# Where the second unit's key products and the inverses' steps are called in a hybrid decoder kernel

## The chip, the cores and the metric

The kernel runs on one core of a Trainium2 chip. The metric is the device time of one execution in microseconds (us). The core has five engines with a queue of instructions each: TensorE (PE in the profile, its weight loads PEld), VectorE (DVE), ScalarE (ACT), GpSimd (POOL) and SyncE (SP), whose queue issues the DMAs. Each queue is worked off in order; semaphores let one engine wait for another or for a DMA. Results of TensorE land in PSUM banks, everything else lies in SBUF.

## What is computed

Two layers, each with three branches over the same normalised input: a state space mixer (SSD), latent attention (MLA) and a gated delta net (GDN). Each branch is projected, gated and summed; then come an output projection and a feed-forward part. The change concerns the delta net's preparation, which runs beside the state space branch's projection:

```python
def gated_delta_chunked(q, k, v, g, beta):
    ...
    decay = jnp.exp(jnp.where(incl, g[..., :, None] - g[..., None, :], -jnp.inf))
    kb = k * beta[..., None]
    a_mat = jnp.where(strict, jnp.einsum('bhcld,bhcmd->bhclm', kb, k) * decay, 0.0)
    rhs = jnp.concatenate([v * beta[..., None], kb * jnp.exp(g)[..., None]], axis=-1)
    sol = lax.linalg.triangular_solve(a_mat + jnp.eye(L, dtype=jnp.float32), rhs,
                                      left_side=True, lower=True)
...
def hybrid_layer(...):
    ...
    mixed = g_ssd * (y_ssd @ w_ssd_out) + g_mla * (y_mla @ w_mla_out) + g_gdn * (y_gdn @ w_gdn_out)
    h = x + mixed @ w_out
```

The sequence has 512 tokens and the model 1024 channels. The delta net has 8 value heads on 4 key heads; its products of keys with keys (`a_mat`) have to be inverted before the scan over the sequence can start.

## The kernel before

Every large product is done three times with operands split into a high and a low part (`mm3`, lines L182 to L184), so that the sum of three fast matmuls has nearly full precision. The split of weights is a cast on ScalarE (`whi`, L154) and a subtraction on VectorE (`wlo`, L155), both ranked as urgent. Weights come by DMA into `wraw` (two buffers, L161); `whi` and `wlo` have four buffers each.

`dense_F` walks the weights of one product in pieces of two blocks of 128 input channels. For two column tiles of 128 it then issues 2 x 2 x 3 = 12 matmuls of 128x128 by 128x512. One such piece is called a row here. After each row `dense_F` calls the function given as `after`. `out_proj` runs, for each of four pieces `dp` of 256 channels, the gate's product (four rows, operand `xh`/`xl`) and the branch's projection (four rows, operand `yh`/`yl`), 32 rows in all. For the state space projection `after` is `between`, which counts the rows from 0. The delta net's query product of unit 0 (`key_tiles(2 * u, between)` in `gdn_unit`) has four more rows, 32 to 35, that call it too.

The delta net's eight heads are done in two units of four. `gdn_matrix(u)` consists of

- `key_tiles`: the product for two key tiles, then convolution and SiLU (ScalarE and VectorE) into `ft`;
- the products of keys with keys (L834, 128x128), evacuated into `wk0` to `wk3` (L838, L839);
- their norms: a power on POOL (L843) and a few short operations on VectorE;
- 16 products with the decays, which are loaded into `eE` (L854), into `nt` (tag `tok`, L857), and four stores of its diagonal blocks to `d_n` (L861).

`gdn_blocks` loads the blocks of both units (L873) and inverts them by 31 steps of two operations each on VectorE (L879, L880). It stores the result and its transpose to `d_x` and `d_y` (L885) and loads them back in another order into `wk` (L888). `gdn_inverse` returns nine closures, the steps: `first` for each unit (64 small matmuls at L913, from `wk`), `second` for each unit (L929, L930) and five of `last_doubling` (L949, L951). `between` calls one of them behind each row from a given one on.

No engine's order is written out by hand. The program is traced as it is written, and a scheduler then orders each engine's instructions ahead of time: an instruction's rank is its place in the program (raised for code in `tc.high_priority()`), and the scheduler takes, engine by engine, the instruction of best rank among those whose inputs and buffers it expects to be ready by its own estimate of durations. The order is fixed from then on; on the chip an engine whose next instruction has no data yet waits.

Of the kernel before, what the change touches and what calls it, by code (L numbers as in the profile page):

```python
# [55 lines left out]
def hybrid_kernel(ctx, tc, a, out, depth=2, taps=None):  # L56
# [4 lines left out]
    def mk(pl, shape, dt, tag, bufs=None):  # L61
        return pl.tile(shape, dt, tag=tag, name=f"{tag}_{next(uid)}", bufs=bufs)
# [8 lines left out]
    def bc_mid(ap, n):  # L71
        sh = list(ap.shape)
        return ap.unsqueeze(1).to_broadcast([sh[0], n] + sh[1:])

    def bc_last(ap, n):
        sh = list(ap.shape)
        return ap.unsqueeze(len(sh)).to_broadcast(sh + [n])
# [15 lines left out]
    def sm_bank():  # L93
        return mk(ps_sm, [P, 512], F32, "sm")
# [70 lines left out]
    def weights(w2d, c0, n, K, hold=None, raw0=None):  # L165

        kt = min(1024 // n, K // P)  # L170
        step = 512 // n
        for k0 in range(0, K // P, kt):
            given = raw0 is not None and k0 == 0
            raw = raw0 if given else weights_raw(w2d, c0, n, k0, kt)
            for q in range(0, kt, step):
                hi, lo = split_half(raw[:, q * n : (q + step) * n], hold and hold[k0 + q], not given)
                v = lambda x: x.rearrange("p (k n) -> p k n", n=n)
                yield k0 + q, v(hi), v(lo)
# [7 lines left out]
    def dense_F(gen, cols, K, xh, xl, mid=None, banks=None, after=None):  # L186

        pss = banks or [acc_bank() for _ in cols]
        last = K // P - 1
        if mid:
            gen = list(gen)
            for i, hf in enumerate(HALVES):
                for ps, c in zip(pss, cols):
                    for k0, wh, wl in gen:
                        for k in range(wh.shape[1]):  # L200
                            kk = k0 + k
                            mm3(ps[:, hf], wh[:, k, c], wl[:, k, c], xh[kk][:, hf], xl[kk][:, hf], kk == 0, kk == last)
                if i == 0:
                    mid()
            return pss
        for k0, wh, wl in gen:
            for ps, c in zip(pss, cols):
                for k in range(wh.shape[1]):
                    a_, b_ = wh[:, k, c], wl[:, k, c]
                    mm3(ps[: a_.shape[1], :], a_, b_, xh[k0 + k], xl[k0 + k], k0 + k == 0, k0 + k == last)  # L210
            if after:
                after()
        return pss

    def tiles(n):
        return [slice(i, i + P) for i in range(0, n, P)]
# [134 lines left out]
    for ly in range(depth):  # L351
# [198 lines left out]
        for hp in range(4):  # L550
# [67 lines left out]
            for j in range(2):  # L618
# [3 lines left out]
                for t in range(T):  # L622
                    n = max(256, (t + 1) * P)
# [9 lines left out]
                    n = (t + 1) * P  # L633
# [11 lines left out]
                for kbs in ((0,), (1,), (3, 2)):  # L645
                    ps = sm_bank()
                    n = 0
# [158 lines left out]
        def gconv_silu(ps, c, o):  # L806
            conv_silu(ps, [gconv(j, c) for j in range(4)], None, o)

        def key_tiles(c0, after=None):

            res = [mk(br, [P, S], F32, "ft", 6) for _ in range(2)]
            for i, ps in enumerate(dense_F(weights(w_in, O_GQ + c0 * P, 256, D), tiles(256), D, xh, xl, after=after)):
                gconv_silu(ps, c0 + i, res[i])
            return res
# [6 lines left out]
                    seg_exp(e, t, 16 + 4 * u)  # L821
                    sync.dma_start(d_e[u, t], e)

        def gdn_matrix(u):

            hd0 = 16 + 4 * u
            kT = key_tiles(4 + 2 * u)
            ssq = mk(sp, [P, 2, T], F32, "gss", 2)
            gks = []
            for t in range(T):  # L830
                tok = slice(t * P, (t + 1) * P)
                pg = sm_bank()
                for i in range(2):
                    pe.matmul(pg[:, i * P : (i + 1) * P], kT[i][:, tok], kT[i][:, tok], start=True, stop=True)  # L834
                gk = mk(br, [P, 2, P], F32, f"wk{t}")
                for i in range(2):

                    dve.scalar_tensor_tensor(gk[:, i], hv(pg)[:, i], 1.0, ident, ALU.mult, ALU.mult, accum_out=ssq[:, i, t : t + 1])  # L838
                dve.tensor_tensor(gk, hv(pg)[:, 0:2], bc_mid(nstrict, 2), ALU.mult)  # L839
                gks.append(gk)  # L840
            dve.tensor_scalar(ssq, ssq, 4.0 * EPS, None, ALU.add)
            ork = mk(sp, [P, 2, T], F32, "gork", 2)
            pool.tensor_tensor(ork.rearrange("p i t -> p (i t)"), ssq.rearrange("p i t -> p (i t)"), phalf[:, :8], ALU.pow)  # L843
            dve.tensor_scalar(ork, ork, 0.5, None, ALU.mult)
            rk2 = mk(sp, [P, 2, T], F32, "grk", 2)
            dve.reciprocal(rk2, ssq)
            cc = mk(sp, [P, T, 4], F32, "gcc", 2)
            for i in range(2):
                dve.tensor_tensor(cc[:, :, 2 * i : 2 * i + 2], beta[:, :, 4 * u + 2 * i : 4 * u + 2 * i + 2],
                                  bc_last(rk2[:, i, :], 2), ALU.mult)  # L850
            nt = mk(br, [P, T, 4, P], F32, "tok", 5)
            for t in range(T):
                e = mk(br, [P, 4, P], F32, "eE", 4)
                sync.dma_start(e, d_e[u, t])  # L854
                gk = gks[t]
                for h in range(4):
                    dve.scalar_tensor_tensor(nt[:, t, h], e[:, h], cc[:, t, h : h + 1], gk[:, h // 2], ALU.mult, ALU.mult)  # L857
            ntf = nt.rearrange("p t h n -> p (t h) n")
            for b in range(4):
                sl = slice(32 * b, 32 * b + 32)  # L860
                sync.dma_start(d_n[u][:, b].rearrange("h i j -> i h j"), ntf[sl, :, sl])  # L861
            cd = mk(sp, [P, T, 4], F32, "gcd", 2)
            dve.tensor_tensor(cd, cc, dec[:, 1, :, hd0 : hd0 + 4], ALU.mult)
            return kT, ork, cc, cd, nt

        def gdn_blocks():

            wk = mk(br, [P, 2, 32, 32], F32, "tok", 5)
            nb, xb = wk[:, 0], wk[:, 1]
            sync.dma_start(nb, d_n.rearrange("u h b i j -> (u h b) i j"))  # L873
            xf = xb.rearrange("p i j -> p (i j)")
            pool.memset(xf, 0.0)
            pool.memset(xf[:, ::33], 1.0)
            for m in range(31):
                pd = mk(br, [P, 31 - m, m + 1], F32, "gQ", 2)
                dve.tensor_tensor(pd, bc_last(nb[:, m, m + 1 :], m + 1), bc_mid(xb[:, m, : m + 1], 31 - m), ALU.mult)  # L879
                dve.tensor_tensor(xb[:, m + 1 :, : m + 1], xb[:, m + 1 :, : m + 1], pd, ALU.add)  # L880
            xbt = nb
            dve.tensor_copy(xbt, xb.rearrange("p i j -> p j i"))
            res = [[], []]
            for i, (src, d_) in enumerate(((xb, d_x), (xbt, d_y))):
                sync.dma_start(d_.rearrange("u h b i j -> (u h b) i j"), src)  # L885
                for u in range(2):
                    c = mk(br, [P, 16, 32], F32, f"wk{2 * i + u}")
                    sync.dma_start(c, d_[u].rearrange("h b i j -> (b i) h j"))  # L888
                    res[u].append(c)
            return res  # L890
# [70 lines left out]
        def gdn_unit(u, kT, ork, cc, cd, Yt, yh, yl):  # L961
            hd0 = 16 + 4 * u
            qT = key_tiles(2 * u, between)
            pss = sm_bank()
            for i in range(2):
# [111 lines left out]
        ssd_group(1, *ys)  # L1077
        out_proj(a["w_mla_out"][ly], 1, *y_mla, br, (2, 3))
        d_n, d_x, d_y = (mk(dr, [2, 16, 4, 32, 32], F32, n, 2) for n in ("d_n", "d_x", "d_y"))
        mats = [gdn_matrix(u) for u in range(2)]  # L1080
        blocks = gdn_blocks()
        steps = gdn_inverse([m[4] for m in mats], blocks)

        rows = itertools.count()

        def between():
            if next(rows) >= 24 and steps:
                steps.pop(0)()

        out_proj(a["w_ssd_out"][ly], 0, *ys, br, after=between)  # L1090
        yg = hilo_tags(lp, "y")
        for u in range(2):
# [312 lines left out]
```

## Time and profile before

| | us |
|---|---|
| median of three timed executions | 2307.58 |
| their range | 2307.19 to 2308.72 |
| the profiled execution's own time | 2309.95 |
| its span, first to last instruction | 2308.2 |
| mean granted TensorE clock in it | 0.996 |

In the views of the trace a line of the timeline gives the start and the duration in us, the engine, the line of the program, the operation, output<-input and a count. In square brackets stand the idle time of the engine ahead of it and what ended that time. A line of the waits gives who waited for whom, then the total in us, the number of times and the longest. The granted clock is a share of full speed.

### The profile page before, as it was taken

Reading aid. Unit: us, or ns where it says so; the run is one execution under the profiler, and the core shown is the slowest. Engines: PE = TensorE matmul, PEld = TensorE weight load, DVE = VectorE, ACT = ScalarE, POOL = GpSimd, SP = SyncE. Lnnn points to the kernel's source line nnn. Section 1 sums busy time; section 2 is a strip of 40 time slices with the busy share of each in tenths; the row PEclk is TensorE's granted clock in tenths of the full one; section 3 lists DMA queues with packets and bytes.
Section 4 is the critical chain, followed back from the end, with each engine's and each line's share of the span. In section 5 each row is a group of like instructions: output and inputs, shape, how many; then the busy total and the mean of one; then the engine's idle time right before and its main releaser. Section 6 shows DMA issues by size and latency. Waiting matters only on the chain.

```text
span 2308.2 us, 32276 instructions
## 1 busy us (share of the span) xinstructions
PE 2272.9 (98%) x11810; PEld 1867.7 (81%) x11810; DVE 1645.9 (71%) x3256; ACT 1202.0 (52%) x2509; POOL 59.4 (3%) x74
## 2 busy tenths in 40 slices
PE   9999999999999999999999999999999999999998
PEld 8888787878887888888888887878788877888886
DVE  7777566875666778767867765668657667778668
ACT  6766644333443455554657666443334435645545
POOL 0000000000000000000000000000000000000000
PEclk9999999999999999999999999999999999999999
DMA  4223633442223233233132236334422241432231
GB/s 142 80 74 101 192 101 119 131 126 83 78 78 134 95 137 110 75 117 119 47 103 79 71 110 192 101 110 146 120 82 83 65 164 55 152 113 101 92 110 46
DMA packets 220032, 244.16 MB, mean 106 GB/s; under 512 B 34256, under 2 KB 172384, under 8 KB 219872
## 3 DMA queue, kind: packets, MB, share of 16 engines
q1 hardware_dynamic: 219872, 242.09, 33.3%
q8 instruction: 93, 1.52, 0.3%
q14 instruction: 67, 0.55, 0.1%
HBM read 225.60 MB, written 11.74 MB: 103 GB/s over the span
## 4 chain that ended last, share of the span: by engine, by line
PE 88%; DVE 6%; ACT 1%; DMA 1%; POOL 1%; issue 1%; SPq 0%; DVEq 0%; POOLq 0%; ACTq 0%
PE acc L182 22%; PE acc L183 22%; PE acc L184 22%; PE sm L182 3%; PE sm L184 3%; PE sm L183 3%; DVE wlo L155 2%; PE sm L752 1%; DVE tok L880 1%; PE sm L650 1%; DVE gQ L879 1%; PE sm L761 1%; PE sm L1037 1%; POOL gms L259 1%; ACT whi L154 1%
## 5 line engine op out<-in xcount | busy, mean ns | idle before, releaser
L154 ACT CAST whi<-wraw 128x512 fp32r<-128x512 f32 (+1 forms) x536 | 329.9, 618 | 546.1 <-PE acc L183 382.7
L155 DVE TENSOR_TENSOR wlo<-wraw,whi 128x512 fp32r<-128x512 f32 (+1 forms) x536 | 365.2, 686 | 347.9 <-ACT whi L154 341.4
L184 PE MATMUL acc<-xh,wlo 128*128 128x512 f32 (+1 forms) x1344 | 523.9, 390 | 0.0
L182 PE MATMUL acc<-xh,whi 128*128 128x512 f32 (+1 forms) x1344 | 523.4, 390 | 0.0
L183 PE MATMUL acc<-xl,whi 128*128 128x512 f32 (+1 forms) x1344 | 523.0, 389 | 0.0
L183 PEld LDWEIGHTS acc<-xl,whi 128*128 128x128 f32 x1344 | 253.7, 189 | 48.3 <-DVE xl L255 0.7
L184 PEld LDWEIGHTS acc<-xh,wlo 128*128 128x128 f32 x1344 | 253.6, 189 | 47.9
L182 PEld LDWEIGHTS acc<-xh,whi 128*128 128x128 f32 x1344 | 253.3, 189 | 48.1 <-ACT xh L254 0.4
L154 ACT CAST whi<-wr 128x512 fp32r<-128x512 f32 x168 | 104.3, 621 | 107.8 <-PE acc L183 47.7
L183 PE MATMUL acc<-yl,whi 128*128 128x512 f32 x384 | 151.4, 394 | 0.0
L182 PE MATMUL acc<-yh,whi 128*128 128x512 f32 x384 | 150.7, 396 | 0.0
L184 PE MATMUL acc<-yh,wlo 128*128 128x512 f32 x384 | 149.9, 390 | 0.0
L155 DVE TENSOR_TENSOR wlo<-wr,whi 128x512 fp32r<-128x512 f32 x168 | 113.2, 686 | 35.6 <-ACT whi L154 34.7
L691 DVE SCALAR_TENSOR_TENSOR ckl<-acc,pc,ckl 128x511 f32<-128x511 f32 (+2 forms) x168 | 120.3, 743 | 15.5 <-ACT ckl L687 8.2
L182 PEld LDWEIGHTS acc<-yh,whi 128*128 128x128 f32 x384 | 71.6, 188 | 16.1 <-ACT yh L254 1.7
L184 PEld LDWEIGHTS acc<-yh,wlo 128*128 128x128 f32 x384 | 72.2, 188 | 14.5
L183 PEld LDWEIGHTS acc<-yl,whi 128*128 128x128 f32 x384 | 72.2, 188 | 13.8
L183 PE MATMUL acc<-wlo,xh 128*128 128x512 f32 (+1 forms) x208 | 79.9, 384 | 0.0
L184 PE MATMUL acc<-whi,xl 128*128 128x512 f32 (+1 forms) x208 | 79.5, 384 | 0.0
L182 PE MATMUL acc<-whi,xh 128*128 128x512 f32 (+1 forms) x208 | 79.5, 384 | 0.0
L1145 DVE TENSOR_TENSOR h<-h,acc 128x512 f32<-128x512 f32 x120 | 76.9, 679 | 0.1
L454 ACT ACTIVATE eE<-eE,cum 128x128 f32<-128x128 f32 x192 | 63.1, 390 | 22.7 <-DMA eE<-d_c 19.7
(453 smaller groups left out, 4552.2 us busy)
## 6 DMA issues: line engine op xcount, KB each, us to landing
wraw<-in_w_in_dram SPq DMA_DIRECT2D x144, 512.0 KB, 3.4
wraw<-in_w_up_dram SPq DMA_DIRECT2D x64, 512.0 KB, 3.6
wr<-in_w_down_dram SPq DMA_DIRECT2D x32, 1024.0 KB, 5.0
eE<-d_c SPq DMA_DIRECT2D x48, 256.0 KB, 4.0
wraw<-in_w_mla_out_dram SPq DMA_DIRECT2D x16, 512.0 KB, 3.3
eE<-d_e SPq DMA_DIRECT2D x32, 256.0 KB, 2.8
wraw<-in_w_ssd_out_dram SPq DMA_DIRECT2D x16, 512.0 KB, 3.3
wraw<-in_w_gdn_out_dram SPq DMA_DIRECT2D x16, 512.0 KB, 3.3
```

The lines of the kernel that those rows point to most:

```text
L154: act.copy(hi, raw)
L155: dve.tensor_tensor(lo, raw, f32(hi), ALU.subtract)
L182: pe.matmul(o, ah, bh, start=start, stop=False, skip_group_check=more)
L183: pe.matmul(o, ah, bl, start=False, stop=False, skip_group_check=more)
L184: pe.matmul(o, al, bh, start=False, stop=stop, skip_group_check=more)
L259: pool.tensor_tensor(o, o, (exp if exp is not None else nhalf)[:, : o.shape[1]], ALU.pow)
L454: act.activation(o[:, i], o[:, i], AF.Relu, scale=-1.0, bias=cum[:, t, h0 + i : h0 + i + 1])
L650: pe.transpose(ps[:, n : n + P], pn[t][:, kb * P : (kb + 1) * P], ident)
L691: dve.scalar_tensor_tensor(acc[:, d:], ps[:, : S - d], taps_[3 - d], acc[:, d:], ALU.mult, ALU.add)
L752: pe.matmul(py[64 * i : 64 * i + 64, c * P : (c + 1) * P], xd[:, t, h * 64 : (h + 1) * 64], e2[h // 4][:, h % 4, :], start=True, stop=True)
L761: pe.matmul(po[:, c * P : (c + 1) * P], st[:, c * P : (c + 1) * P], ctl[:, tok], start=True, stop=True)
L1145: dve.tensor_tensor(hs_, hs_, ps[t], op)
```

## The change

The second unit's key tiles are still computed ahead of the projection, right behind the first unit's matrix. The rest of the second unit's matrix, the inversion of the blocks and the making of the steps are called from `between` behind row 1, that is, from within the projection. The steps are called from row 26 on instead of row 24, so that the nine lie behind rows 26 to 34 instead of 24 to 32. What is computed stays the same.

```diff
-        def gdn_matrix(u):
+        def gdn_matrix(u, kT):
 
             hd0 = 16 + 4 * u
-            kT = key_tiles(4 + 2 * u)
             ssq = mk(sp, [P, 2, T], F32, "gss", 2)
...
-        mats = [gdn_matrix(u) for u in range(2)]
-        blocks = gdn_blocks()
-        steps = gdn_inverse([m[4] for m in mats], blocks)
+        mats = [gdn_matrix(0, key_tiles(4))]
+        k1 = key_tiles(6)
+        steps = []
 
         rows = itertools.count()
 
         def between():
-            if next(rows) >= 24 and steps:
+            n = next(rows)
+            if n == 1:
+                mats.append(gdn_matrix(1, k1))
+                steps.extend(gdn_inverse([m[4] for m in mats], gdn_blocks()))
+            if n >= 26 and steps:
                 steps.pop(0)()
```

## The prediction

> **What bounds the kernel now.** I read the page first, then the waits of TensorE, then the order of its instructions around the change in both layers, then the granted clock in short stretches.
>
> ```profile
> span 2308.2 us, 32276 instructions
> PE 2272.9 (98%) x11810; PEld 1867.7 (81%) x11810; DVE 1645.9 (71%) x3256; ACT 1202.0 (52%) x2509; POOL 59.4 (3%) x74
> ...
> PE 88%; DVE 6%; ACT 1%; DMA 1%; POOL 1%; issue 1%; SPq 0%; DVEq 0%; POOLq 0%; ACTq 0%
> ```
>
> TensorE is busy 2272.9 of 2308.2 us and has 88% of the chain that ended last. The change adds and removes no matmul, so it can win only what TensorE stands idle, or runs slow, near the moved code. Its waits there are two kinds:
>
> ```profile
> PE sm L913 <- DMA wk<-d_x: 2.7, 2, 1.8
> ...
> PE sm L834 <- DVE ft L263: 1.7, 2, 0.8
> ```
>
> L913 is the first step of the inverses (once in each layer it waits, 2.7 us in all); L834 is the second unit's key products (0.84 us in each layer). I number the projection's rows from 0, as the counter does. Layer 0 around the first step:
>
> ```profile
> 484.69 0.39 PE L182 MATMUL acc<-yh,whi 128*128 128x512 f32 x1
> ...
> 495.57 0.39 PE L182 MATMUL acc<-xh,whi 128*128 128x512 f32 x1
> ...
> 499.65 0.39 PE L182 MATMUL acc<-xh,whi 128*128 128x512 f32 x1
> 501.79 1.49 PE L913 MATMUL sm<-wk,tok 32*32 32x32 f32 x64 [1.76 <-DMA wk<-d_x]
> 503.21 0.80 PE L183 MATMUL acc<-xl,whi 128*128 128x512 f32 x1
> ...
> 505.64 1.92 PE L913 MATMUL sm<-wk,tok 32*32 32x32 f32 x64
> 507.49 0.80 PE L182 MATMUL acc<-xh,whi 128*128 128x512 f32 x1
> ...
> 512.84 0.22 PE L929 MATMUL sm<-wk,ft 32*32 32x32 f32 x2
> ```
>
> The operand changes from yh to xh where a gate product starts, every four rows. From 484.69 (row 20) to 495.57 (row 24) are 48 matmuls in 10.88 us: **0.2267 us a matmul, 2.72 us a row** of 12. So row 24 ends at 498.29, and the step, called behind row 24, stands 7 matmuls into row 25 ((499.65 - 498.29) / 0.2267 + 1). The second L913 stands 5 matmuls later, just behind row 25, and L929 12 later, behind row 26: these at their own calls. An instruction thus stands at its call, or later if its inputs were expected later. The same place in layer 1:
>
> ```profile
> 1646.61 0.39 PE L182 MATMUL acc<-xh,whi 128*128 128x512 f32 x1
> 1647.96 1.20 PE L913 MATMUL sm<-wk,tok 32*32 32x32 f32 x64 [0.96 <-DMA wk<-d_x]
> 1649.09 0.50 PE L183 MATMUL acc<-xl,whi 128*128 128x512 f32 x1
> ...
> 1654.52 0.22 PE L929 MATMUL sm<-wk,ft 32*32 32x32 f32 x2
> ```
>
> The same work, from the first L913 to the first L929, takes 512.84 - 501.79 = 11.05 us in layer 0 and 1654.52 - 1647.96 = 6.56 us in layer 1. Busy time in stretches (busy us and count of PE, PEld, DVE, ACT, POOL, then the granted clock) says why:
>
> ```profile
> 500.00:501.79 1.79, 0.03 (x1) 0.00 (x0) 0.00 (x0) 0.02 (x1) 0.00 (x0) 1.00 0.86 138
> 501.79:503.21 1.42, 1.42 (x64) 1.35 (x65) 0.00 (x0) 1.22 (x2) 0.00 (x0) 0.74 1.23 194
> 503.21:505.64 2.43, 2.43 (x9) 1.49 (x5) 0.70 (x1) 1.51 (x3) 0.00 (x0) 0.50 1.08 170
> ...
> 512.84:516.90 4.06, 4.06 (x110) 3.27 (x109) 1.37 (x2) 2.19 (x5) 0.00 (x0) 1.00 0.01 4
> ...
> 1648.00:1650.45 2.45, 2.45 (x70) 1.91 (x70) 0.64 (x1) 2.39 (x5) 0.00 (x0) 1.00 1.26 198
> ```
>
> Behind layer 0's idle time the clock falls to 0.50 until about 512.8; in layer 1 it stays at 1.00. The wait of 1.76 us therefore drags **11.05 - 6.56 = 4.49 us** behind it.
>
> What the step waits for, on VectorE and SyncE's queue:
>
> ```profile
> 455.07 0.33 SPq L873 DMA_DIRECT2D tok<-d_n  x1
> 461.44 0.18 DVE L879 TENSOR_TENSOR gQ<-tok 128x31 f32<-128x31 f32 x1
> ...
> 492.80 0.18 DVE L880 TENSOR_TENSOR tok<-tok,gQ 128x31 f32<-128x31 f32 x1
> 493.38 0.45 SPq L885 DMA_DIRECT2D d_x<-tok  x1
> 498.25 2.26 SPq L888 DMA_DIRECT2D wk<-d_x  x2
> 501.77 0.62 ACT L907 COPY tok<-wk 32x512 f32<-32x512 f32 x1 [2.89 <-DMA wk<-d_x]
> 505.32 0.62 ACT L154 CAST whi<-wraw 128x512 fp32r<-128x512 f32 x1 [0.78 <-PE acc L183]
> ```
>
> 31 steps on VectorE, a store at 493.38, the load issued at 498.25 and landed by 501.77: 8.4 us of round trip, and TensorE waits at its end.
>
> **The change part by part.** First, **the key products of unit 1** are called behind row 1 instead of ahead of row 0. Where they stand now:
>
> ```profile
> 433.11 0.39 PE L184 MATMUL acc<-xh,wlo 128*128 128x512 f32 x1
> 434.34 0.94 PE L834 MATMUL sm<-ft 128*128 128x128 f32 x6 [0.84 <-DVE ft L263]
> ...
> 440.71 0.39 PE L182 MATMUL acc<-yh,whi 128*128 128x512 f32 x1
> ```
>
> Row 4 starts at 440.71 (xh to yh); 21 of the 48 matmuls of rows 0 to 3 lie between L834 and that, so 27 lie ahead: the products already stand 3 matmuls behind the end of row 1. Their call moves past 24 matmuls that run ahead of them anyway, so I expect the same place and take 0. Bounds: the wait of 0.84 us vanishes in both layers (-1.68), or everything behind slips by two rows (the last rival). What else it issues, queue by queue:
>
> ```profile
> 399.61 17.01 SPq L161 DMA_DIRECT2D wraw<-in_w_in_dram  x4
> 421.53 9.32 SPq L161 DMA_DIRECT2D wraw<-in_w_ssd_out_dram  x2
> ...
> 436.05 2.42 SPq L854 DMA_DIRECT2D eE<-d_e  x3
> ...
> 446.59 0.99 POOL L906 MEMSET tok<- 32x512 f32 x2
> ```
>
> On SP it moves 4 loads of eE, 4 stores to d_n, and with the blocks the load of d_n, 2 stores and 4 loads of wk, all past one weight load, that of rows 0 and 1. The two loads at 421.53 and later are those of rows 4 to 7, so the last two of the four before them, issued by 416.6, are those of rows 0 to 3: nearly 20 us ahead of unit 1's first eE load at 436.05. This order stays as well: 0. POOL gets the power of L843 and the clearings; the L906 clearing belongs to the first step, called behind row 24, and yet ran at 446.59, 55 us ahead of the step. A call's place ranks work that is ready at the same time; it doesn't hold back work alone in its queue.
>
> Second, **the steps begin behind row 26.** The first L913 moves by the 5 matmuls left of row 25 and the 12 of row 26: 17 x 0.2267 = 3.85 us. Without waiting TensorE is free for it in layer 0 at 501.79 - 1.76 + 3.85 = 503.88 us, and the data, whose chain does not depend on TensorE's place, is there at 501.79: 2.1 us to spare. Layer 1: 1647.96 - 0.96 + 3.85 = 1650.85 against 1647.96, 2.9 to spare. So both waits go, and the slow stretch with them:
> 1.76 + 0.96 + 4.49 = **7.21 us**.
>
> On ScalarE the copies of L907 stay where they are ready, at 501.77, with the casts for coming rows queued behind. The cast at 505.32 is row 29's (whi has four buffers, so a cast follows the row four ahead of its own). It and VectorE's 0.69 us are over by some 507. With the change TensorE reaches row 29 at 503.88 + 1.13 + 2.72 + 1.13 + 2.72 + 1.1 = 512.7. Some 5 us of cover, so 0; were it gone, the excess would be a wait of TensorE.
>
> **The late end.** The nine steps now lie behind rows 26 to 34; three instead of one fall into unit 0's query product. Layer 1, where the last step now stands:
>
> ```profile
> 1678.78 1.14 PE L951 MATMUL sm<-tok,kt 64*64 64x64 f32 x16
> 1679.85 0.50 PE L182 MATMUL acc<-xh,whi 128*128 128x512 f32 x1
> ...
> 1695.18 0.95 PE L969 MATMUL sm<-ct,ft 128*128 128x1 f32 x8
> ```
>
> Two rows on, that step starts near 1679.85 + 5.44 = 1685.3, some 10 us ahead of L969, the first work of the unit after its query product, which waits for the query's convolution. The cost is 0 while the rows cover it; without them the last step and its copy, about 1.14 + 0.6 = 1.7 us a layer, would be in sight.
>
> The sum against the profiled execution's own time is 2309.95 - 7.21 = 2302.74 us (span 2300.97). That execution lies 2.37 us above the median 2307.58; on the median the forecast is **2300.4 us** (-0.31%).
>
> **The rivals.**
> (1) **Timed runs without the slow stretch.** The clock fell in one layer of two, so it may be a matter of chance. The three times, 2307.19 to 2308.72, lie closer than 4.49, so they all have it or all lack it. If they lack it, 1.76 + 0.96 = 2.72 is won: **2304.9**. For it: layer 1 at 1.00 after 0.96 us. Against it: the profiled execution without the stretch would be at 2305.46, 2.1 below the timed ones, which would make profiling a gain.
> The Trainium skill, "TensorE: Matmul & The Clock Gate", Part 1, states that the clock is cut after about 3.4 us without work, in a window that runs free of the kernel. By its length 1.76 us would not cut the clock and only 2.72 us could be won; the row with 0.50 disagrees, and the free window would leave each run to chance.
> (2) **Given back.** The wait goes, but one of the later steps, now among query rows, meets a wait that idles TensorE as long as this one: 1.76 + 4.49 return in one layer, 0.96 stays won: **2306.6**. For it: VectorE and ScalarE take their work in order. Against it: steps remain one row apart.
> (3) **The chain slips (slower).** If unit 1's products and all behind them do move by two rows, the data lands 5.44 us later, at 507.23 and 1653.40, against TensorE at 503.88 and 1650.85: waits of 3.35 and 2.55 us, each long enough for a slow stretch. 3.35 + 2.55 + 2 x 4.49 = 14.88 instead of 7.21: **2315.3**. It decides from a slip of 2.1 us on in layer 0. For it: the call is written behind row 1. Against it: the products already stand behind row 1.
>
> **How the numbers follow.** The forecast has 0.56, rival 1 0.24, rival 2 0.09, rival 3 0.11. The likeliest case alone runs from 2298.7 (the 1.68 of L834 won too) to 2301.9; the range goes on over rivals 1 and 2 to 2307.5 and leaves out rival 3 and some tails. About 0.2% (4.6 us) is what a measurement of this kernel tells from no change: the forecast lies beyond it, rivals 1 and 2 within, rival 3 beyond on the other side. With the tails: faster 0.55, same 0.35, slower 0.10.
>
> **What would show it.** Right: no wait of L913 for wk in either layer, the first L913 behind 12 more full matmuls of row 26, clock 1.00 throughout that stretch, L834 still 27 matmuls into the projection, a span near 2301. Wrong: a later start of the 31 steps relative to row 4, or a clock of 0.50 anywhere past the start, or a new wait of TensorE in the query rows.

## The result and the profile after

| | before | after |
|---|---|---|
| median of 20 timed runs, us | 2310.12 | 2305.23 |
| mean of them, us | 2310.25 | 2305.29 |
| lowest and highest, us | 2306.89, 2314.17 | 2303.88, 2307.16 |
| span of the profiled execution, us | 2308.2 | 2303.2 |

The ratio is 0.9978, with a 95% interval from 0.9972 to 0.9984: faster by 4.9 us. The three times known ahead (median 2307.58) lie in the lower part of the 20.

TensorE's waits after (who waited for whom, us in total, times, longest), where the loads of `wk` had 2.7 us:

```profile
PE sm L1017 <- DVE tok L1014: 3.5, 8, 0.5
...
PE sm L833 <- DVE ft L263: 1.7, 2, 0.8
```

No line of the list names `wk` any more; the wait of the key products is what it was (the changed kernel's lines from 833 on are numbered one lower). TensorE's timeline of the changed kernel, layer 0:

```profile
435.85 0.94 PE L833 MATMUL sm<-ft 128*128 128x128 f32 x6 [0.84 <-DVE ft L263]
...
505.31 1.20 PE L912 MATMUL sm<-wk,tok 32*32 32x32 f32 x64
506.44 0.50 PE L182 MATMUL acc<-xh,whi 128*128 128x512 f32 x1
...
509.39 1.20 PE L912 MATMUL sm<-wk,tok 32*32 32x32 f32 x64
510.52 0.50 PE L182 MATMUL acc<-yh,whi 128*128 128x512 f32 x1
```

There is no bracket at L912: the step no longer waits. The second one is followed by yh, that is, it stands at the end of row 27. ScalarE's timeline there:

```profile
503.17 0.62 ACT L906 COPY tok<-wk 32x512 f32<-32x512 f32 x1 [2.79 <-DMA wk<-d_x]
503.80 0.62 ACT L907 COPY tok<-wk 32x512 f32<-32x512 f32 x1
504.45 0.62 ACT L154 CAST whi<-wraw 128x512 fp32r<-128x512 f32 x1
```

The data is there at 503.17, TensorE comes at 505.31: 2.14 us to spare, where 2.1 were worked out. The cast that is queued behind the copies runs at 504.45. Busy times and granted clock of the same place (the columns as in the prediction):

```profile
500.00:505.31 5.31, 5.31 (x24) 4.13 (x22) 0.90 (x2) 2.48 (x5) 0.00 (x0) 1.00 0.92 155
505.31:510.52 5.21, 5.21 (x142) 4.36 (x141) 2.86 (x6) 4.54 (x8) 0.00 (x0) 1.00 1.03 250
510.52:525.00 14.48, 14.48 (x259) 11.65 (x255) 6.74 (x10) 6.38 (x11) 0.00 (x0) 1.00 0.28 81
```

TensorE is busy throughout and the clock stays at 1.00. The only stretch at 0.50 in this profile is its end, from 2296.26 us to the last instruction, when TensorE's last matmul is over; every profile of this case ends so, 4.1 to 7.0 us long, and it costs no matmul anything. The late end of the steps, in layer 1:

```profile
1679.00 1.14 PE L950 MATMUL sm<-tok,kt 64*64 64x64 f32 x16
1680.08 0.50 PE L182 MATMUL acc<-xh,whi 128*128 128x512 f32 x1
...
1689.96 0.94 PE L968 MATMUL sm<-ct,ft 128*128 128x1 f32 x8
```

The last step is over 9.9 us ahead of the first work behind the query product, and no line of TensorE's waits is new there.

Between the profiled executions lie 5.0 us, not 7.21. From L834 of unit 1 to the work behind the query product, layer 0 became 6.30 us shorter (434.34 to 553.47 before, 435.85 to 548.68 after; 1.76 + 4.49 = 6.25 were forecast), and layer 1 from its first key product on 1.02 shorter (0.96). But the profiled execution after had lost 1.5 us by 435.85, ahead of everything changed, and 0.6 more between the layers.

### The profile page after: what moved, and what is told of

The parts are those of the page before. It is cut to its first block, busy times and chain, and to the rows that moved or that the text cites. A ratio compares the mean times of both kernels' runs of the same rounds, so it can differ in the third digit from the quotient of the medians.

```text
span 2303.2 us, 32278 instructions
## 1 busy us (share of the span) xinstructions
PE 2268.3 (98%) x11810; PEld 1864.5 (81%) x11810; DVE 1646.7 (71%) x3256; ACT 1201.6 (52%) x2509; POOL 59.4 (3%) x74
## 4 chain that ended last, share of the span: by engine, by line
PE 91%; DVE 4%; ACT 2%; POOL 1%; DMA 1%; issue 1%; SPq 0%; DVEq 0%; POOLq 0%; ACTq 0%
PE acc L182 23%; PE acc L183 23%; PE acc L184 23%; PE sm L184 3%; PE sm L182 3%; PE sm L183 3%; DVE wlo L155 1%; PE sm L752 1%; PE sm L650 1%; ACT whi L154 1%; PE sm L1036 1%; POOL gms L259 1%; PE yt L666 1%; PE sm L290 1%; PE sm L630 1%
```

## The experiments

Theory A: the first edit does nothing, the second removes the waits of L913; theory C: the slow stretch behind the wait is a matter of chance in each execution. Each experiment was timed beside the kernel before on its chip, and medians are compared only between kernels timed together. The ratio with its interval is an estimate of its own; it differs from the quotient of the two medians by up to 0.0008.

**Each edit alone.** First the move alone, with the steps from row 24:

```diff
-            if n >= 26 and steps:
+            if n >= 24 and steps:
```

> The first edit alone (unit 1's products called behind row 1, steps from row 24 as before). Theory A (the call's place only ranks work, and the products already stood behind row 1): every engine's order is that of the kernel before, so no change: ratio 1.000 within 0.1%, L913 waits of about 1.8 and 1.0 us in the two layers. Theory B (the edit has a part in the gain): 1 to 3 us faster. On the slow-clock stretch, theory C (a matter of chance, run by run): the runs scatter over about 7 us, and the mean clock takes different values from run to run, 0.002 apart for each stretch; theory D (always one stretch): scatter of about 3 us as in the changed kernel, and one clock.

Measured: 2310.37 us in 12 runs against 2309.64, ratio 1.0004 (0.9995 to 1.0012). With line numbers and buffer numbers left out, the order of instructions in the trace is that of the kernel before on each of the five engines, line for line. Then the late start alone, in the kernel before:

```diff
-            if next(rows) >= 24 and steps:
+            if next(rows) >= 26 and steps:
```

> The second edit alone (steps from row 26, unit 1's products called where they were). Theory A: every engine's order is that of the changed kernel, so its whole gain: 4.9 us less than before (ratio 0.9978), no L913 wait, all runs within about 3.5 us. Theory B (both edits have a part): 2 to 4 us less than before, and an L913 wait in one of the layers.

Measured: 2304.80 us, ratio 0.9979 (0.9970 to 0.9987), 2304.2 to 2305.6 in 11 runs, and no wait of L913. Its order is that of the changed kernel on every engine. Theory A holds: the first edit has no part in it.

TensorE's timeline of the move alone, whose order is that of before, shows the same wait with another stretch behind it; the granted clock follows in windows:

```profile
503.72 1.20 PE L912 MATMUL sm<-wk,tok 32*32 32x32 f32 x64 [1.82 <-DMA wk<-d_x]
504.85 0.62 PE L183 MATMUL acc<-xl,whi 128*128 128x512 f32 x1
...
508.78 0.50 PE L182 MATMUL acc<-xh,whi 128*128 128x512 f32 x1
...
1648.90 1.20 PE L912 MATMUL sm<-wk,tok 32*32 32x32 f32 x64 [1.24 <-DMA wk<-d_x]
```

```profile
503.72:505.10 1.38, 1.38 (x65) 1.34 (x66) 0.00 (x0) 1.34 (x3) 0.00 (x0) 0.99 1.19 188
505.10:508.50 3.40, 3.40 (x57) 2.45 (x58) 1.73 (x3) 2.30 (x4) 0.00 (x0) 0.50 1.08 179
508.50:512.00 3.50, 3.50 (x56) 2.68 (x54) 2.04 (x5) 3.06 (x6) 0.00 (x0) 1.00 0.85 254
```

Here the clock is at 0.50 for 3.4 us; in the profile of before it was some 10.2 us, from 502.5 to 512.7. The timed runs bear it out. The kernel before ran 35 times, and its time goes with the mean clock of the run:

| mean clock of the run | runs | median us |
|---|---|---|
| 0.999 | 10 | 2307.82 |
| 0.998 | 12 | 2309.46 |
| 0.997 | 10 | 2311.54 |
| 0.996 | 3 | 2313.52 |

Theory C holds; "always one stretch" (theory D) falls. The late start alone had 0.999 in 10 of 11 runs, with a median of 2304.77. Between runs of clock 0.999 lie 2307.82 - 2304.77 = **3.05 us**, and the two waits in the profile of the move alone are 1.82 + 1.24 = **3.06 us**. The other 4.84 - 3.05 = 1.8 us between the medians are put down to slow clock. The mean clock is a coarse sign, though: the end of the span alone brings it to 0.998 or 0.999 (the profiled execution of the changed kernel has 0.998 with no other stretch), and a stretch of 3.4 us at half clock takes off only 0.0007 more.

**Half the distance:** the kernel before with the steps from row 25.

```diff
-            if next(rows) >= 24 and steps:
+            if next(rows) >= 25 and steps:
```

> Kernel before with the steps from row 25. The first step moves by 5 matmuls, 1.13 us, where 17 matmuls are the whole edit. By the waits: layer 0 keeps 1.76 - 1.13 = 0.63 us of wait, layer 1 none, 2.09 of the 2.72 us won. Theory C (the slow stretch needs an idle time longer than the 0.84 us that L834 shows without one): no stretch any more, so 0.6 us slower than the changed kernel, 4.3 us faster than before, scatter about 3 us. Rival (any wait at this place, with the small matmuls behind it, brings the stretch): 0.6 + up to 4.5 us slower than the changed kernel in layer 0, runs scattered over 7 us.

Measured: 2305.86 us, 1.1 us over the late start, ratio 0.9981 (0.9973 to 0.9990). TensorE's waits:

```profile
PE sm L913 <- DMA wk<-d_x: 0.9, 1, 0.9
```

Layer 1 waits no more, layer 0 for 0.88 us, 0.25 more than worked out. The 11 runs lie from 2304.89 to 2307.53 with clocks of 0.998 and 0.999, against 0.996 to 0.999 before: no sign of long stretches behind the shorter wait, and none in its profile.

**Calling the steps earlier:** the kernel before with the steps from row 20.

```diff
-            if next(rows) >= 24 and steps:
+            if next(rows) >= 20 and steps:
```

> Kernel before with the steps called from row 20 instead of 24. Theory A (an instruction stands at its call or later, where its inputs are expected): the first L913 stays 7 matmuls into row 25 with the same wait of 1.8 and about 1 us, the following steps stand closer behind each other; time that of the kernel before within 2 us, runs scattered over some 7 us. Rival (the call's place rules): the first step stands behind row 20, 55 matmuls or 12.5 us earlier, and TensorE waits that much longer in each layer: 20 us slower or more.

Measured: 2326.75 us in 6 runs against 2310.64, ratio 1.0062 (1.0046 to 1.0078); the runs lie from 2320.01 to 2331.30 with clocks from 0.995 down to 0.989. Its timeline and windows:

```profile
503.17 1.20 PE L913 MATMUL sm<-wk,tok 32*32 32x32 f32 x64 [1.76 <-DMA wk<-d_x]
...
1656.53 1.20 PE L913 MATMUL sm<-wk,tok 32*32 32x32 f32 x64 [1.23 <-DMA wk<-d_x]
```

```profile
504.50:525.00 20.50, 20.50 (x341) 16.09 (x342) 7.22 (x12) 8.81 (x15) 0.00 (x0) 0.50 0.32 76
525.00:535.00 10.00, 10.00 (x96) 8.03 (x93) 2.77 (x5) 4.08 (x7) 0.00 (x0) 1.00 0.19 54
...
1658.00:1678.70 20.70, 20.33 (x343) 15.98 (x343) 7.22 (x12) 8.68 (x15) 0.00 (x0) 0.51 0.31 73
```

The place is as theory A said: the first step still stands 7 matmuls into row 25, with the same two waits, though it is called four rows earlier. The time is not: the clock stays at 0.50 for some 20.5 us in both layers. What differs is that at most 4 full matmuls stand between the steps that follow, up to 525 us, instead of 5 and then 12. In the slow stretch TensorE is busy, but for 12.1 of the 20.5 us with matmuls of 32x32 and 64x64. Two stretches of 20.5 us at half clock cost up to 2 x 10.25 = 20.5 us; the kernel is 16.1 slower than one that has some of them too.

**More full matmuls behind the first step:** the kernel before, with no step behind row 25.

```diff
-            if next(rows) >= 24 and steps:
+            n = next(rows)
+            if n >= 24 and n != 25 and steps:
```

> Kernel before, with no step called behind row 25: the first step stays 7 matmuls into row 25, the next comes 17 full matmuls later instead of 5, and all after it one row later. Theory A (the slow stretch needs idle time and, close to it, much time in small matmuls; full matmuls behind the wait end it): the waits of L913 stay, 1.8 and 1.0 to 1.2 us, but stretches are rarer or shorter: 1 to 2 us less than the kernel before, clocks of the runs mostly 0.998 or 0.999. Rival (the idle time alone brings the stretch): no change, clocks down to 0.996 in several runs.

Measured: 2309.15 us against 2308.62, ratio 0.9998 (0.9989 to 1.0006). Its 11 runs lie from 2308.22 to 2311.38 with clocks from 0.997 to 0.999, the 27 of before beside it from 2306.80 to 2313.34 down to 0.996. The scatter is narrower, but the 1 to 2 us that theory A forecast did not come: the mean is the same (2309.29 and 2309.40), and the lowest run is 1.4 us slower. Its profile shows no cost of the later steps: from unit 1's first key product (in layer 1 from unit 0's) to the work behind the query product it takes 2.00 us longer than the changed kernel in layer 0 and 1.06 us in layer 1, and its two waits are 1.92 and 1.00 us. Why its lowest run lies higher stays open. Its longer wait is the longest of all at this step, and the clock stays at 1.00 behind it:

```profile
503.57 1.20 PE L913 MATMUL sm<-wk,tok 32*32 32x32 f32 x64 [1.92 <-DMA wk<-d_x]
```

```profile
503.57:508.78 5.21, 5.21 (x82) 4.20 (x82) 2.77 (x6) 5.10 (x9) 0.00 (x0) 1.00 1.10 195
```

**The slip itself:** the changed kernel with the products behind row 3.

```diff
-            if n == 1:
+            if n == 3:
```

> Changed kernel with unit 1's products called behind row 3, steps from row 26 as there: the slip of the last rival, made on purpose. The products come to stand 48 matmuls into the projection instead of 27, 4.76 us later; the first step stays where it is. Theory A (the data of the first step follow the products): 4.76 us eat the 2.1 us that TensorE has to spare in layer 0 and the 2.9 us in layer 1, so L913 waits 2.7 and 1.9 us; L834's wait goes (-1.7); slow stretches by chance, now longer waits than in the kernel before, 1.7 to 5.1 us each. Sum: 3 us slower than the changed kernel without a stretch, up to 13 with two. Rival (VectorE has idle time and catches up): no L913 wait, 1.7 us faster than the changed kernel.

Measured: 2303.80 us in 5 runs against 2310.64, ratio 0.9969 (0.9957 to 0.9981); the changed kernel beside it:

> The changed kernel once more, beside the two others of this chip and for the clock of each run: ratio 0.998 to the kernel before, no run with a clock under 0.997, all within about 3.5 us.

2305.56 us, ratio 0.9975 (0.9965 to 0.9984), 8 runs from 2304.14 to 2307.33, all clocks 0.998 or 0.999. The slip does not wait at L912, so theory A fell here. It is 1.76 us below the changed kernel, as the rival said, but its waits don't give that much: the 1.68 us for `ft` are gone, and 1.46 us for a PSUM bank have come. Its timelines, TensorE and then VectorE and SyncE's queue:

```profile
423.16 1.50 PE L833 MATMUL sm<-ft 128*128 128x128 f32 x12
...
440.84 1.50 PE L833 MATMUL sm<-ft 128*128 128x128 f32 x12
444.22 0.71 PE L833 MATMUL sm<-ft 128*128 128x128 f32 x4 [0.73 <-DVE wk L838]
```

```profile
442.42 0.17 DVE L862 TENSOR_TENSOR gcd<-gcc,dec 128x16 f32<-128x16 f32 x1
443.11 0.29 DVE L837 SCALAR_TENSOR_TENSOR wk<-sm,ct 128x128 f32<-128x128 f32 x1
...
463.96 0.18 DVE L878 TENSOR_TENSOR gQ<-tok 128x31 f32<-128x31 f32 x1
```

```profile
495.65 0.45 SPq L884 DMA_DIRECT2D d_x<-tok  x1
```

and the same of the changed kernel:

```profile
421.92 1.50 PE L833 MATMUL sm<-ft 128*128 128x128 f32 x12
...
442.66 0.61 PE L833 MATMUL sm<-ft 128*128 128x128 f32 x4
```

```profile
441.24 0.17 DVE L862 TENSOR_TENSOR gcd<-gcc,dec 128x16 f32<-128x16 f32 x1
441.32 0.28 DVE L837 SCALAR_TENSOR_TENSOR wk<-sm,ct 128x128 f32<-128x128 f32 x1
...
462.94 0.18 DVE L878 TENSOR_TENSOR gQ<-tok 128x31 f32<-128x31 f32 x1
```

```profile
494.88 0.45 SPq L884 DMA_DIRECT2D d_x<-tok  x1
```

Counted from unit 0's first key product, the 31 steps start at 463.96 - 423.16 = 40.80 us with the products 21 matmuls later, and at 462.94 - 421.92 = 41.02 us in the changed kernel: not a bit later. Their result is stored at 495.65 - 423.16 = 72.49 and 494.88 - 421.92 = 72.96 us. In the changed kernel the products are finished early for nothing: VectorE is still at unit 0's matrix (its last operation is L862 at 441.24) and evacuates the first three only then (L837 at 441.32); the fourth, whose bank has to come free, starts at 442.66. L862 comes 19.3 us after the first key product in both kernels, and the fourth product moved by 0.3 us only (442.66 - 421.92 = 20.74 against 444.22 - 423.16 = 21.06). So VectorE's work seems to set the chain; no run moved that work, so this is read from the traces and not tested.

**Looking for more:** two kernels should also remove the 0.84 us at L834, with the products behind row 2 and the steps from row 27:

```diff
-            if n == 1:
+            if n == 2:
...
-            if n >= 26 and steps:
+            if n >= 27 and steps:
```

> Changed kernel with the products behind row 2 and the steps from row 27. The products move by 9 matmuls, 2.04 us, more than the 0.84 us they wait in each layer. If that wait is only a matter of place: no wait of L834 for ft in unit 1, 1.7 us less than the changed kernel, 6.6 less than before. Rival (the chain of the blocks slips by up to 2 us with it and the last step, now behind row 35, runs into the query's convolution): the gain is given back, time that of the changed kernel within 1 us.

Measured: 2305.11 us beside 2304.80 of the late start. The wait for `ft` is gone, but the fourth product waits 0.48 us for its bank behind VectorE's L838 in each layer. Then the same with row 4 (`n == 4`), beside the slip once more:

> Changed kernel with unit 1's products behind row 4 (60 matmuls into the projection) and the steps from row 27. The products then wait neither for ft nor for a PSUM bank (the slip had 0.73 us of that in each layer, since VectorE was still at unit 0's matrix at 442.4 us): 1.7 us less than the changed kernel. The last of them comes 15 matmuls, 3.4 us, later than in the changed kernel, against 2.1 + 2.7 us to spare, so no wait of L913. Rival (some wait stays, or the data is late): time of the changed kernel or more.

> The products behind row 3, steps from row 26, once more beside the two others: it was 6.8 us under the kernel before in 5 runs, the changed kernel 5.1 in 8 on the same chip. By its waits it should win only 1.68 - 1.46 = 0.2 us over the changed kernel; if 1 us or more shows again, something else was won.

Both beside 2308.62 of the kernel before. Row 4: 2305.62 us, ratio 0.9981 (0.9973 to 0.9990); the slip: 2304.12, ratio 0.9977 (0.9968 to 0.9986). In the first no wait of L833 is left and none of L912 comes, as expected, and yet its median isn't lower: runs from 2303.88 at clock 0.999 to 2309.26 at 0.996. Two new idle times stand in its profile, both inside the `second` steps of layer 0, and the profile shows nothing that ended them:

```profile
PE sm L928 <- issue: 0.6, 1, 0.6
...
PE sm L929 <- issue: 0.4, 1, 0.4
```

It also shows a slow stretch at another place, an older wait of both kernels (timeline, then windows); the first profile of the slip has one of the same length behind the same wait:

```profile
63.79 1.23 PE L492 MATMUL sm<-ct,yh 128*128 128x128 f32 x8 [1.10 <-DVE yh L487]
```

```profile
62.30:65.68 3.38, 2.28 (x19) 1.71 (x17) 1.74 (x5) 1.91 (x5) 1.02 (x1) 1.00 0.40 150
65.68:69.09 3.41, 3.41 (x10) 2.73 (x10) 2.42 (x5) 1.61 (x3) 1.14 (x1) 0.50 0.00 0
```

The slip's second result, in 11 runs, is 4.50 us under the kernel before, where the first was 6.84 in 5 and the changed kernel's 5.08 in 8: the extra gain didn't show again. None of the three beats the changed kernel by more than the intervals.

## Why the prediction came out as it did

The direction is right, and the time, 2305.23, lies in the range. But it lies outside what the likeliest case alone allowed (2298.7 to 2301.9), and the range holds it only because it went on over rivals 1 and 2. That it came out next to rival 1's 2304.9 is luck: that rival took the level of before 2.5 us too low and the gain 2.2 us too low, and the two errors cancel. Step by step:

- **The first edit costs and wins nothing:** right. The order is the same on all engines, and alone it measures 1.0004.
- **The second edit removes both waits of L913:** right, with 2.14 us to spare in layer 0 for the 2.1 worked out. The term 1.76 + 0.96 = 2.72 was 3.06 in another execution, and 3.05 us showed between runs of clock 0.999.
- **The slow stretch, 4.49 us:** this is the term of the sum that was mis-sized. The profile of before held one long draw; in the profiles of this order (before and the move alone) it is some 10.2 and some 3.4 us long in layer 0 and absent in layer 1. In the timed runs it is worth about 4.96 - 2.72 = 2.2 us on the mean, half of the term, and 1.8 between the medians of the kernel before and the late start alone. So 7.2 us became 4.9.
- **"They all have it or all lack it"** (rival 1): wrong, and with it the choice between 7.21 and 2.72. Three runs within 1.53 us said little about a quantity that spreads 35 runs of the same kernel over four values of the clock. That rival's mechanism, chance, was the true one; its time, 2304.9, supposed that the known runs had no stretch. That they lay low among 20 (2307.58 against 2310.12) moved the absolute time up by some 2.5 us, as the mis-sized term did by 2.3.
- **The late end costs nothing:** right; 9.9 us of cover were left.
- **Rival 2, given back:** no new wait in the query rows.
- **The signs of being wrong:** "a clock of 0.50 anywhere past the start" was drawn too wide. The changed kernel's profile has such a stretch at its end, and so has that of before.
- **Rival 3, the slip:** it didn't happen, and its price was wrong too. The data of the step does not follow the first products: a call two rows later still left the chain where it was. The price rested on one instruction's place; the traces show VectorE still at the first unit's matrix when the products are ready.

## What to carry to other kernels

When a program is ordered by a scheduler, the place of a call only ranks work that is ready: before judging a move, find where the instructions stand now; a call moved up to that place changes nothing. A wait of TensorE near small matmuls cost its own length here and more by chance, so look at the time and the mean clock of several executions before taking the one in the profile as its price. A few repeats of a kernel that scatters over 0.3% are a poor base for an absolute time.

## What the runs showed of the hardware

The clock of TensorE fell to 0.50 behind idle times of 1.10 and 1.11 us at L492 (row 4 and the slip), and of 1.23, 1.76, 1.76 and 1.82 us at the first step, with transposes (L492) or matmuls of 32x32 next to them. It did not in the profiled executions behind 0.84 us at the key products, behind 0.88, 0.96, 1.00, 1.24 and 1.92 us at the first step, behind 1.10 to 1.16 us at L492 in the 22 other places, or behind 1.67 us at L630 (the move alone), where matmuls of 128x128 by 128x256 follow. So the length of the idle time alone doesn't decide.

The stretches lasted about 3.4, 10.2 and 20.5 us, 1, 3 and 6 times the same span. Within one execution all changes of the clock lie whole multiples of 3.413 us apart: 502.46 and 2301.28 us in the kernel before are 527 of them apart, 504.56, 525.04 and 1658.27 us in the start from row 20 are 6 and 332. If this grid is laid back over each profile from the fall at its end, the waits of 1.23, 1.76, 1.76 and 1.82 us at the first step lie whole within one interval, and those of 1.24 and 1.92 us, behind which the clock stayed, are cut by a boundary into 0.88 + 0.36 and 1.27 + 0.65 us. The chance of theory C may thus be where the grid lies to the wait; six waits are too few to show it.

The longest stretch came where the small matmuls of the steps lay closest together: TensorE was never idle in the 20.5 us of layer 0 and yet stayed at half clock, so what counts is not idle time alone. The Trainium skill, "TensorE: Matmul & The Clock Gate", Part 1, gives a free-running window of about 3.4 us; the lengths agree with it. It asks for a whole idle window to lower the clock and one busy window to raise it. The runs show less than that for the one (1.1 us idle in row 4's profile) and, with small matmuls, more for the other (20.5 us). How much activity the window asks for, none of the runs measured.
